# Where the two halves of an output projection run: beside the attention, or after it beside the norms

## The chip, the core and the metric

The kernel runs on one core of a Trainium2 chip. The metric is the device time of one execution in microseconds (us), median of the runs. A NeuronCore has TensorE (PE: matmuls and transposes; its weight loads are listed as PEld), VectorE (DVE), ScalarE (ACT), GpSimd (POOL) and SyncE (SP), which here issues the DMA transfers. Each engine works off its own queue in order and waits on semaphores.

## The reference, cut to what matters

One decoder layer over 1024 tokens and 16 meta tokens, d_model 1024. Two token mixers (retention, and sparse attention with a top-256 choice of keys) each give 512 columns; together they are mapped by one output projection, added to the residual, normed, and put through an MLP.

```python
y = jnp.concatenate([y_ret, y_dsa], axis=-1).astype(h.dtype)
h = h + y @ w_out[l]
u = rmsnorm(h, norm2_w[l]).astype(h.dtype)
h = h + jnp.square(jax.nn.relu(u @ w_ff1[l])) @ w_ff2[l]
```

All of it is in float32. The kernel reaches that precision with pairs: each operand is split into a high half (a float32r copy, made by ACT) and a low half (the rest, made by DVE or GpSimd), and a product is three matmuls, high by high, low by high and high by low.

## The kernel before

The tokens are eight blocks of 128 rows. The stages follow each other: norm and projections with the indexer and the top-k (0 to about 425 us), the attention (to about 652), the rest of the output projection with the second norm (to about 713), and the MLP (to the end). The MLP works with sums and differences of quarters of its operands (seven products in place of eight, names `u1` to `u7`), and reads W1 in pieces of 512 KB (`w1_load`, name `wr`), from which DVE makes sums (`sum`, L952) and ACT and DVE make halves (`wh`, `wl`, L955 and L956).

The attention runs in rounds `u` = 2 i + g, for block i and half g of the heads. In a round `attend_p` computes the scores and the softmax of (i, g), while `attend_v` of the round before transposes the probabilities (L607) and multiplies them by the values (L617, L619).

The output projection is cut into 16 pieces, (half of the columns, block). A piece needs `out_prep`, which loads the retention part of y from memory (`yr`), transposes it on PE (L654), and splits both parts into `ys` (ACT L657, and DVE or GpSimd L658); two sets of `ys` take turns. Then `out_mm` does 24 matmuls (L669 to L671), and DVE adds the residual `hp` and so drains the result (L674), which goes to memory as `hd`. `out_w` loads and splits half of the weights; only one half is held at a time. In what order the pieces come is said by a table, `pieces`, for the rounds, and by a list, `todo`, for the stretch after the attention:

```python
pieces = {4: [(0, 0)], 5: [(0, 1)], 7: [(0, 2)], 9: [(0, 3)], 10: [(1, 0)], 11: [(1, 1)], 12: [(1, 2)],
          13: [(1, 3)], 14: [(1, 4)], 15: [(1, 5)]}
...
todo = [(1, 7), (0, 4), (0, 5), (0, 6), (0, 7)]
```

Piece (1, 6) runs beside the last `attend_v`. So ten pieces and that one, eleven in all, lie within the attention, and five after it; the first half of the weights is loaded twice.

`norm2` turns a row block of h into operands of the MLP: a square with its sum on ACT (L852), a root on GpSimd (L142), the scaled row `un` on DVE (L854), eight transposes on PE (L862), and then halves of sums and differences. For blocks 0 to 3 that is light (two more instructions on DVE), for blocks 4 to 7 heavy (six more on DVE). Blocks 0 to 3 were normed beside the last `attend_v` (`norms_a`), blocks 4 to 7 in the stretch after it (`norm2_b`, `norm_step`). The first four products of the MLP (`u4` and `u2`, twice) need only blocks 0 to 3; the next one (`u3`) needs all eight.

The code is written with generators that `spread` takes in turns. A scheduler of the framework then sets the order of each engine's queue from its own forecast of times, so the order in the queues is not the one written; the section on the change shows it where it matters.

Of the kernel before, what the change touches and what calls it, by code (L numbers as in the profile page):

```python
# [18 lines left out]
D = 1024  # L19
# [3 lines left out]
NB = 8  # L23
# [58 lines left out]
def layer(ctx, tc, x, meta, norm1_w, w_in, ret_w, q_w, k_w, rel, w_out, norm2_w, w1, w2,  # L82
# [552 lines left out]
    hd = dr.tile([128, NB, D], F32, name="hd")  # L635

# [4 lines left out]
    def out_prep(ch, b):  # L641
        yr = wp.tile([128, 512], F32, tag="rl", name="yr", bufs=2)
        nc.sync.dma_start(yr, yrd[:, b])
# [6 lines left out]
        hp = at["hp"][oc[0] % 2]  # L650
        nc.sync.dma_start(hp, x[128 * b:128 * b + 128, 512 * ch:512 * ch + 512])
        tp = psB()
        for c in range(4):
            nc.tensor.transpose(tp[:, 128 * c:128 * c + 128], yr[:, 128 * c:128 * c + 128], ident)  # L654
        ys = [a.rearrange("p (c n) -> p c n", c=4) for a in at["y"][oc[0] % 2]]
        for k, src in enumerate((tp.rearrange("p (c n) -> p c n", c=4), ydsa[b])):
            nc.scalar.activation(ys[k], src, AF.Copy)  # L657
            (nc.gpsimd if k else nc.vector).tensor_tensor(ys[2 + k], src, ys[k].bitcast(F32), op=ALU.subtract)  # L658
        return ys, hp
# [4 lines left out]
    def out_mm(ch, b, ys, hp):  # L664
        hs, ls = ow[0]
        ps = psB()
        for d in range(8):
# [3 lines left out]
            nc.tensor.matmul(ps, yh, ls[d], start=False, stop=d == 7)  # L671
            yield
        dst = hrow[0][:, b % 2, :512] if b >= 4 and ch == 0 else hp
# [144 lines left out]
    while runs:  # L818
        for g in list(runs):
            try:  # L820
# [6 lines left out]
    pieces = {4: [(0, 0)], 5: [(0, 1)], 7: [(0, 2)], 9: [(0, 3)], 10: [(1, 0)], 11: [(1, 1)], 12: [(1, 2)],  # L827
              13: [(1, 3)], 14: [(1, 4)], 15: [(1, 5)]}
# [20 lines left out]
    def norm2(b, src, u):  # L849
# [20 lines left out]
        def temp():  # L870
            if b < 4:
                return wp.tile([128, 4, 128], F32, tag="wr", name="ut", bufs=3)
            return p2["p"].tile([128, 4, 128], F32, tag="yd", name="ut", bufs=4)
# [20 lines left out]
    def norms_a():  # L894
        nr = [page([128, 2, D], F32, "nr") for _ in range(2)]
        for b in range(4):
            nc.sync.dma_start(nr[b % 2][:, 0], hd[:, b])
            yield from norm2(b, nr[b % 2][:, 0], nr[b % 2][:, 1])
            yield

    spread((NB + 1, attend_v(NB - 1, 1)), (9, out_piece(1, 6)), (12, norms_a()))
# [10 lines left out]
    def load_h(b):  # L912
        nc.sync.dma_start(hrow[0][:, b % 2, 512:], hd[:, b, 512:])
# [213 lines left out]
    for k, (ch, b) in enumerate(todo):  # L1127
        if k == 1:
            out_w(0, True)
# [74 lines left out]
```

## Time and profile before

| | |
|---|---|
| median of 3 runs | 1323.49 us (1321.75 to 1327.82) |
| the profiled execution | 1322.03 us, span 1320.3 us |
| PE busy | 1254.5 us, 95% |
| DVE busy | 1038.5 us, 79% |
| ACT busy | 767.3 us, 58% |
| GpSimd busy | 253.5 us, 19% |
| mean granted TensorE clock | 0.986 |
| moved by DMA | 153.46 MB |

The span runs from the first to the last instruction; the profiled execution's own time is 1.7 us longer. PE's busy time counts the whole duration of matmuls that overlap in the array, so a full PE is read from the distance between starts. A granted clock of 1.00 is 2.4 GHz, 0.5 is 1.2 GHz.

### The profile page before, as it was taken

Reading aid. Unit: us, or ns where it says so; the run is one execution under the profiler, and the core shown is the slowest. Engines: PE = TensorE matmul, PEld = TensorE weight load, DVE = VectorE, ACT = ScalarE, POOL = GpSimd, SP = SyncE. Lnnn points to the kernel's source line nnn. Section 1 sums busy time; section 2 is a strip of 40 time slices with the busy share of each in tenths; the row PEclk is TensorE's granted clock in tenths of the full one; section 3 lists DMA queues with packets and bytes.
Section 4 is the critical chain, followed back from the end, with each engine's and each line's share of the span. In section 5 each row is a group of like instructions: output and inputs, shape, how many; then the busy total and the mean of one; then the engine's idle time right before and its main releaser. Section 6 shows DMA issues by size and latency. Waiting matters only on the chain. (4 is left out here: it accounts for less than half of the span.)

```text
span 1320.3 us, 18430 instructions
## 1 busy us (share of the span) xinstructions
PE 1254.5 (95%) x6144; PEld 1036.8 (79%) x6144; DVE 1038.5 (79%) x2277; ACT 767.3 (58%) x1588; POOL 253.5 (19%) x298
## 2 busy tenths in 40 slices
PE   5999989999999899999987999999999999999998
PEld 4888867877877677787775888888887888888887
DVE  5589999995458888776769877777778988887875
ACT  6567466887875668565746555554546444444442
POOL 4003472425335333210333000000000200000000
PEclk9999989999999999999997999999999999999999
DMA  8103031202112111212543343443538834444222
GB/s 275 59 17 90 22 91 63 72 9 72 35 55 74 66 62 56 65 47 74 179 149 112 141 159 131 150 159 131 177 144 303 342 141 168 151 144 177 94 96 96
DMA packets 94046, 153.46 MB, mean 116 GB/s; under 512 B 7752, under 2 KB 47856, under 8 KB 90240
## 3 DMA queue, kind: packets, MB, share of 16 engines
q1 hardware_dynamic: 93952, 152.29, 33.4%
q8 instruction: 48, 0.79, 0.2%
q14 instruction: 46, 0.38, 0.1%
HBM read 110.32 MB, written 43.46 MB: 116 GB/s over the span
## 5 line engine op out<-in xcount | busy, mean ns | idle before, releaser
L955 ACT ACTIVATE wh<-ga 128x512 fp32r<-128x512 f32 x144 | 87.3, 628 | 157.6 <-PE psB L1103 142.9
L246 PE MATMUL psA<-wh,uh 128*128 128x512 f32 x376 | 151.7, 404 | 3.5 <-DVE fg L481 2.2
L247 PE MATMUL psA<-wh,ul 128*128 128x512 f32 x376 | 149.2, 397 | 0.0
L248 PE MATMUL psA<-wl,uh 128*128 128x512 f32 x376 | 148.7, 396 | 0.0
L956 DVE TENSOR_TENSOR wl<-ga,wh 128x512 fp32r<-128x512 f32 x144 | 96.5, 686 | 47.4 <-ACT wh L955 46.8
L955 ACT ACTIVATE wh<-sum 128x512 fp32r<-128x512 f32 x128 | 78.7, 625 | 80.1 <-DVE sum L952 75.6
L723 ACT ACTIVATE jk_top<-sc,tcand 128x784 bf16<-128x784 f32 (+2 forms) x93 | 98.3, 1057 | 23.9 <-DVE tcand L793 19.8
L1103 PE MATMUL psB<-wh,wl 128*128 128x512 f32 x280 | 109.0, 389 | 0.9 <-DVE wl L956 0.9
L1104 PE MATMUL psB<-wl,wh 128*128 128x512 f32 x280 | 108.9, 389 | 0.0
L1102 PE MATMUL psB<-wh 128*128 128x512 f32 x280 | 106.8, 389 | 0.0
L956 DVE TENSOR_TENSOR wl<-sum,wh 128x512 fp32r<-128x512 f32 x128 | 87.5, 684 | 6.2 <-ACT wh L955 6.2
L246 PEld LDWEIGHTS psA<-wh,uh 128*128 128x128 f32 x376 | 71.3, 190 | 17.6 <-DVE fg L481 1.9
L1022 POOL COPY ga<-wl 128x1 f32<-128x1 f32 x8 | 6.6, 826 | 404.8 <-DVE wl L956 361.4
L248 PEld LDWEIGHTS psA<-wl,uh 128*128 128x128 f32 x376 | 71.2, 190 | 13.9
L247 PEld LDWEIGHTS psA<-wh,ul 128*128 128x128 f32 x376 | 71.4, 190 | 12.2
L718 DVE TENSOR_SCALAR_CACHE_REDUCE jk_cnt<-sc,tcand 128x400 bf16<-128x400 f32 (+2 forms) x93 | 70.3, 756 | 1.0
L194 POOL TENSOR_TENSOR wl<-wr,wh 128x512 fp32r<-128x512 f32 x48 | 67.0, 1418 | 18.4 <-ACT wh L189 12.3
L358 ACT ACTIVATE rl<-psB,absw 128x320 f32<-128x320 f32 (+5 forms) x104 | 53.0, 555 | 28.5 <-DVE sc L362 15.9
L1103 PE MATMUL psA<-wh,wl 128*128 128x512 f32 x168 | 65.4, 389 | 0.0
L1104 PE MATMUL psA<-wl,wh 128*128 128x512 f32 x168 | 65.4, 389 | 0.0
L1102 PE MATMUL psA<-wh 128*128 128x512 f32 x168 | 64.9, 389 | 0.0
L952 DVE TENSOR_TENSOR sum<-wr,wr 128x512 f32<-128x512 f32 x48 | 31.7, 686 | 41.5 <-DMA wr<-in_w_ff_dram 36.0
(392 smaller groups left out, 3642.7 us busy)
## 6 DMA issues: line engine op xcount, KB each, us to landing
ga<-hid SPq DMA_DIRECT2D x28, 1024.0 KB, 5.0
wr<-in_w_ff_dram SPq DMA_DIRECT2D x34, 512.0 KB, 5.0
hid<-hs SPq DMA_DIRECT2D x48, 256.0 KB, 2.0
wr<-in_w_in_dram SPq DMA_DIRECT2D x32, 256.0 KB, 3.1
gb<-in_w_ff_dram SPq DMA_DIRECT2D x8, 1024.0 KB, 5.0
ga<-in_w_ff_dram SPq DMA_DIRECT2D x8, 1024.0 KB, 5.9
wr<-in_w_out_dram SPq DMA_DIRECT2D x12, 512.0 KB, 4.1
xt<-in_x_dram SPq DMA_DIRECT2D x8, 512.0 KB, 4.4
```

The source lines that it names most:

```text
L194: e.tensor_tensor(shl, raw, shp.bitcast(F32), op=ALU.subtract)
L246: nc.tensor.matmul(ps[:P, :n], uh, wh, start=d == 0, stop=False)
L247: nc.tensor.matmul(ps[:P, :n], ul, wh, start=False, stop=False)
L248: nc.tensor.matmul(ps[:P, :n], uh, wl, start=False, stop=d == 7)
L358: nc.scalar.activation(r[:, :w], ps[:, :w], AF.Relu, scale=absw[:, i, h:h + 1])
L718: nc.vector.tensor_scalar(jk_[:, :ncol[i]], sc[i], cand[:, j:j + 1], 0.0, op0=ALU.is_ge, op1=ALU.add, accum_out=cnt[:, j:j + 1])
L723: nc.scalar.activation(jk_top[:, :ncol[i]], sc[i], AF.Sign, scale=-1.0, bias=cand[:, j:j + 1], accum_out=cnt[:, j:j + 1])
L955: nc.scalar.activation(view(hi), s, AF.Copy)
L956: nc.vector.tensor_tensor(view(lo), s, view(hi).bitcast(F32), op=SUB)
L1102: nc.tensor.matmul(ps[tb], ah[:, t], bh, start=j == 0 and m not in CONT, stop=False, skip_group_check=True)
L1103: nc.tensor.matmul(ps[tb], al[:, t], bh, start=False, stop=False, skip_group_check=True)
L1104: nc.tensor.matmul(ps[tb], ah[:, t], bl, start=False, stop=j == NO - 1, skip_group_check=True)
```

## The change

The first half of the columns is now done for all blocks before the second: blocks 0 to 5 within the attention (one piece in every second round), block 6 beside the last `attend_v`, and block 7 just after it. The second half follows for all eight blocks, beside the norms of all eight. Each half of the weights is loaded once. The pieces of the second half don't transpose and split y again: while the first half's `out_mm` runs, the four tiles of `ys` are stored to memory (`ysd`, 1 MB per block, L681), and `out_prep` of the second half loads them back (L664). The drain of the second half writes to `hrow` in place, and the first half of the row is fetched from `hd`. `norms_a` is gone. In the line numbers of the changed kernel the drain is L684, `un` is L863, the transposes of a norm are L871, and the heavy differences (`ut`) are L884.

```diff
     def out_prep(ch, b):
-        yr = wp.tile([128, 512], F32, tag="rl", name="yr", bufs=2)
-        nc.sync.dma_start(yr, yrd[:, b])
+
...
         hp = at["hp"][oc[0] % 2]
+        flat = at["y"][oc[0] % 2]
+        ys = [a.rearrange("p (c n) -> p c n", c=4) for a in flat]
+        if ch == 0:
+            yr = wp.tile([128, 512], F32, tag="rl", name="yr", bufs=2)
+            nc.sync.dma_start(yr, yrd[:, b])
+            tp = psB()
+            for c in range(4):
+                nc.tensor.transpose(tp[:, 128 * c:128 * c + 128], yr[:, 128 * c:128 * c + 128], ident)
+            for k, src in enumerate((tp.rearrange("p (c n) -> p c n", c=4), ydsa[b])):
+                nc.scalar.activation(ys[k], src, AF.Copy)
+                (nc.gpsimd if k else nc.vector).tensor_tensor(ys[2 + k], src, ys[k].bitcast(F32), op=ALU.subtract)
+        else:
+            for k in range(4):
+                nc.sync.dma_start(flat[k].bitcast(F32), ysd[:, b, k])
...
             nc.tensor.matmul(ps, yh, ls[d], start=False, stop=d == 7)
+            if ch == 0 and d == 5:
+                for k in range(4):
+                    nc.sync.dma_start(ysd[:, b, k], flat[k].bitcast(F32))
             yield
-        dst = hrow[0][:, b % 2, :512] if b >= 4 and ch == 0 else hp
+        dst = hrow[0][:, b % 2, 512:] if ch else hp
...
-    pieces = {4: [(0, 0)], 5: [(0, 1)], 7: [(0, 2)], 9: [(0, 3)], 10: [(1, 0)], 11: [(1, 1)], 12: [(1, 2)],
-              13: [(1, 3)], 14: [(1, 4)], 15: [(1, 5)]}
+    pieces = {4: [(0, 0)], 6: [(0, 1)], 8: [(0, 2)], 10: [(0, 3)], 12: [(0, 4)], 14: [(0, 5)]}
...
-    spread((NB + 1, attend_v(NB - 1, 1)), (9, out_piece(1, 6)), (12, norms_a()))
+    spread((NB + 1, attend_v(NB - 1, 1)), (9, out_piece(0, 6)))
...
-    todo = [(1, 7), (0, 4), (0, 5), (0, 6), (0, 7)]
+    todo = [(0, 7)] + [(1, b) for b in range(NB)]
     pre = out_prep(*todo[0])
     for k, (ch, b) in enumerate(todo):
         if k == 1:
-            out_w(0, True)
-        nxt = out_prep(*todo[k + 1]) if k < 4 else None
-        spread((8, out_mm(ch, b, *pre)), *([(1.3, norm_step(k + 2))] if k >= 2 else []))
+            out_w(1, True)
+        nxt = out_prep(*todo[k + 1]) if k < NB else None
+        spread((8, out_mm(ch, b, *pre)), *([(1.3, norm_step(b - 1))] if k >= 2 else []))
```

The order on DVE at the first drains that go to `hrow`, that is, of the first blocks that are normed after the attention. Before (the drains are those of blocks 4, 5 and 6; `wr_7814` and `wr_7826` are the second pair of W1 pieces):

```order
L674 TENSOR_TENSOR hrow<-psB,hp 128x512
L952 TENSOR_TENSOR sum<-wr_7814,wr_7826 128x512 x2
L674 TENSOR_TENSOR hrow<-psB,hp 128x512
L854 SCALAR_TENSOR_TENSOR un<-hrow,rs_y,nrow_2078 128x1024
L674 TENSOR_TENSOR hrow<-psB,hp 128x512
L854 SCALAR_TENSOR_TENSOR un<-hrow,rs_y,nrow_2078 128x1024
L877 TENSOR_TENSOR ut<-ut,psB 128x512
```

In the changed kernel, DVE at the same place (the drains are those of blocks 0, 1 and 2; `wr_7749` and `wr_7761` are the second pair):

```order
L684 TENSOR_TENSOR hrow<-psB,hp 128x512
L956 TENSOR_TENSOR wl<-sum,wh 128x512
L863 SCALAR_TENSOR_TENSOR un<-hrow,rs_y,nrow_2078 128x1024
L877 TENSOR_TENSOR u2l<-psB,u2h 128x4x128
L952 TENSOR_TENSOR sum<-wr_7749,wr_7761 128x512 x2
L884 TENSOR_TENSOR ut<-psB,f_7068 128x512
L684 TENSOR_TENSOR hrow<-psB,hp 128x512 x2
L863 SCALAR_TENSOR_TENSOR un<-hrow,rs_y,nrow_2078 128x1024 x2
```

The pair of `sum` now stands behind block 0's `un`, ahead of the drains of blocks 1 to 7.

DVE later, from the first heavy difference of block 4 to the drain of the last piece. Before:

```order
L877 TENSOR_TENSOR ut<-ut,psB 128x512
L877 TENSOR_TENSOR ut<-psB,f_7239 128x512
L956 TENSOR_TENSOR wl<-wr_7678,wh 128x512
L956 TENSOR_TENSOR wl<-sum,wh 128x512
L854 SCALAR_TENSOR_TENSOR un<-hrow,rs_y,nrow_2078 128x1024
L952 TENSOR_TENSOR sum<-wr_7814 128x512
L956 TENSOR_TENSOR wl<-wr_7826,wh 128x512
L956 TENSOR_TENSOR wl<-wr_7814,wh 128x512
L674 TENSOR_TENSOR hrow<-psB,hp 128x512
```

DVE in the changed kernel, from the same instruction to the same drain:

```order
L884 TENSOR_TENSOR ut<-ut,psB 128x512
L884 TENSOR_TENSOR ut<-psB,f_7068 128x512
L956 TENSOR_TENSOR wl<-wr_7620,wh 128x512
L863 SCALAR_TENSOR_TENSOR un<-hrow,rs_y,nrow_2078 128x1024
L956 TENSOR_TENSOR wl<-sum,wh 128x512
L956 TENSOR_TENSOR wl<-wr_7761,wh 128x512
L952 TENSOR_TENSOR sum<-wr_7749 128x512
L877 TENSOR_TENSOR u5l<-psB,u5h 128x4x128
L884 TENSOR_TENSOR ut<-psB,f_7069 128x512
L899 TENSOR_TENSOR f_7068<-psB,f_7068 128x512
L956 TENSOR_TENSOR wl<-wr_7749,wh 128x512
L684 TENSOR_TENSOR hrow<-psB,hp 128x512
```

The same work stands there in nearly the same order. From the first `ut<-ut,psB` (block 4) to the fourth (block 7) DVE's queue has 38 instructions before and 38 after.

SP's queue in the changed kernel, where the reloads of blocks 1 to 3 are issued:

```order
L943 DMA wr_7620<-in_w_ff_dram 128x4x256
L664 DMA ys<-ysd 128x512
L685 DMA hd<-hp 128x512
L943 DMA wr_7749<-in_w_ff_dram 128x4x256
L664 DMA ys<-ysd 128x512 x5
L943 DMA wr_7761<-in_w_ff_dram 128x4x256
L665 DMA hp<-in_x_dram 128x512
L685 DMA hd<-hrow 128x512
L665 DMA hp<-in_x_dram 128x512
L664 DMA ys<-ysd 128x512 x2
L913 DMA hrow<-hd 128x512
```

The reloads take turns with the W1 pieces, the residual and the stores of `hd`, which wait for drains on DVE; before, SP had 256 KB of `yr` per piece here and no transfer of `ys`.

## Rows read from the trace of the kernel before

**Rows 1.** The page: busy time by engine, and PE's granted clock in 40 slices.
```profile
PE 1254.5 (95%) x6144; PEld 1036.8 (79%) x6144; DVE 1038.5 (79%) x2277; ACT 767.3 (58%) x1588; POOL 253.5 (19%) x298
...
PEclk9999989999999999999997999999999999999999
```
**Rows 2.** Stretches: length, then busy time (and instructions) of each engine, clock, DMA.
```profile
660.00:675.00 15.00, 14.94 (x68) 12.05 (x67) 5.14 (x7) 5.84 (x10) 6.38 (x7) 1.00 0.50 163
...
690.00:705.00 15.00, 10.29 (x48) 7.91 (x47) 15.00 (x21) 9.81 (x18) 5.56 (x5) 0.85 0.44 153
...
800.00:900.00 100.00, 100.00 (x443) 82.84 (x442) 75.66 (x120) 52.29 (x95) 0.00 (x0) 1.00 0.42 149
```
**Rows 3.** Timeline of PE: start, duration, instruction, [wait before it and its releaser].
```profile
655.20 0.60 PE L654 MATMUL psB<-ident,yr 128*128 128x128 f32 x4
655.55 0.48 PE L669 MATMUL psB<-wh,ys 128*128 128x512 f32 x1
655.87 0.40 PE L670 MATMUL psB<-wh,ys 128*128 128x512 f32 x1
...
675.79 0.39 PE L671 MATMUL psB<-wl,ys 128*128 128x512 f32 x1
679.42 1.45 PE L862 MATMUL psB<-ident,un 128*128 128x128 f32 x8 [3.24 <-DVE un L854]
...
713.37 0.79 PE L984 MATMUL psB<-u3h,wh 128*128 128x512 f32 x1 [4.83 <-ACT u3h L867]
```
**Rows 4.** Timeline of DVE, 676 to 712.
```profile
676.28 1.29 DVE L952 TENSOR_TENSOR sum<-wr,wr 128x512 f32<-128x512 f32 x2 [3.51 <-issue]
...
678.09 1.27 DVE L854 SCALAR_TENSOR_TENSOR un<-hrow,rs_y,nrow 128x1024 f32<-128x1024 f32 x1
...
681.49 0.68 DVE L877 TENSOR_TENSOR ut<-ut,psB 128x512 f32<-128x512 f32 x1
...
684.53 0.69 DVE L956 TENSOR_TENSOR wl<-sum,wh 128x512 fp32r<-128x512 f32 x1 [1.17 <-ACT wh L955]
...
690.28 0.68 DVE L674 TENSOR_TENSOR hrow<-psB,hp 128x512 f32<-128x512 f32 x1
...
695.68 2.32 DVE L854 SCALAR_TENSOR_TENSOR un<-hrow,rs_y,nrow 128x1024 f32<-128x1024 f32 x1
...
711.98 0.67 DVE L877 TENSOR_TENSOR ut<-ut,psB 128x512 f32<-128x512 f32 x1
```
**Rows 5.** Stretches, each one round of the attention; columns as above.
```profile
480.82:489.11 8.29, 6.97 (x39) 5.02 (x38) 8.01 (x27) 7.42 (x17) 2.25 (x1) 1.00 0.21 65
...
513.12:531.68 18.56, 16.19 (x98) 13.19 (x96) 15.91 (x53) 15.47 (x32) 12.44 (x8) 1.00 0.23 80
...
546.87:563.38 16.51, 16.32 (x98) 13.93 (x98) 12.33 (x43) 10.05 (x20) 3.55 (x2) 1.00 0.14 47
...
580.48:600.00 19.52, 18.46 (x107) 15.32 (x106) 15.13 (x48) 13.12 (x25) 1.28 (x1) 1.00 0.22 72
```
**Rows 6.** Groups by line and shape: count, busy us and mean ns, idle before.
```profile
L658 POOL TENSOR_TENSOR ys<-yd,ys 128x512 fp32r<-128x512 f32 x16 | 21.4, 1339 | 74.4 <-ACT ys L657 74.4
...
L658 DVE TENSOR_TENSOR ys<-psB,ys 128x512 fp32r<-128x512 f32 x16 | 10.9, 686 | 2.8 <-ACT ys L657 2.7
...
L196 DVE SCALAR_TENSOR_TENSOR wl<-wr,rgain,wh 128x512 fp32r<-128x512 f32 x12 | 9.2, 781 | 1.8 <-ACT wh L189 1.7
...
L852 ACT ACTIVATE un<-hrow 128x1024 f32<-128x1024 f32 x4 | 4.2, 1058 | 5.8 <-DVE hrow L674 4.6 <-PE psB L862 0.8 <-DVE ut L877 0.4
```
**Rows 7.** DMA issues (KB, us to landing) at 640 to 720 and 985 to 1060; one stretch.
```profile
wr<-in_w_out_dram SPq DMA_DIRECT2D x4, 512.0 KB, 4.1
...
hrow<-hd SPq DMA_DIRECT2D x4, 256.0 KB, 4.2
...
m<-hd SPq DMA_DIRECT2D x4, 1024.0 KB, 10.2
...
1015.00:1020.00 5.00, 5.00 (x23) 4.13 (x23) 4.49 (x8) 2.20 (x4) 0.00 (x0) 1.00 1.05 428
```

More of the change, by code (lines that the diff above doesn't have):

```diff
@@ L635, in layer @@
     hd = dr.tile([128, NB, D], F32, name="hd")
+    ysd = dr.tile([128, NB, 4, 512], F32, name="ysd")
     ow = {}
@@ L650, in out_prep, with out_mm @@
         hp = at["hp"][oc[0] % 2]
-        nc.sync.dma_start(hp, x[128 * b:128 * b + 128, 512 * ch:512 * ch + 512])
[L652 to L659, printed above, removed]
+        flat = at["y"][oc[0] % 2]
[12 more added lines that the diff above has]
+                nc.sync.dma_start(flat[k].bitcast(F32), ysd[:, b, k])
+        nc.sync.dma_start(hp, x[128 * b:128 * b + 128, 512 * ch:512 * ch + 512])
+        return ys, hp, flat
     def out_w(ch, alt=False):
         ow[0] = load_cols(w_out, [(512 * ch, 512)], alt=alt, gain=rgain)
-    def out_mm(ch, b, ys, hp):
+    def out_mm(ch, b, ys, hp, flat):
         hs, ls = ow[0]
@@ L870, in temp @@
         def temp():
-            if b < 4:
-                return wp.tile([128, 4, 128], F32, tag="wr", name="ut", bufs=3)
             return p2["p"].tile([128, 4, 128], F32, tag="yd", name="ut", bufs=4)
@@ L892, in norm2 @@
             nc.vector.tensor_tensor(g1, tps[1], g1, op=ADD)
[L894 to L899, printed above, removed]
-    spread((NB + 1, attend_v(NB - 1, 1)), (9, out_piece(1, 6)), (12, norms_a()))
+    spread((NB + 1, attend_v(NB - 1, 1)), (9, out_piece(0, 6)))
     att.close()
@@ L912, in load_h @@
     def load_h(b):
-        nc.sync.dma_start(hrow[0][:, b % 2, 512:], hd[:, b, 512:])
+        nc.sync.dma_start(hrow[0][:, b % 2, :512], hd[:, b, :512])
     for m, pg_ in ((5, page), (3, page), (6, page_c), (7, page_c)):
@@ L918, in norm2_b @@
     def norm2_b(b):
-        if b == 4:
+        if b == 0:
             hrow.append(page([128, 2, D], F32, "un"))
@@ L1119, in norm_step @@
         yield
-        if b > 4:
+        if b > 0:
             for _ in norms.pop(b - 1):
@@ L1128, in layer @@
         if k == 1:
-            out_w(0, True)
-        nxt = out_prep(*todo[k + 1]) if k < 4 else None
-        spread((8, out_mm(ch, b, *pre)), *([(1.3, norm_step(k + 2))] if k >= 2 else []))
+            out_w(1, True)
+        nxt = out_prep(*todo[k + 1]) if k < NB else None
+        spread((8, out_mm(ch, b, *pre)), *([(1.3, norm_step(b - 1))] if k >= 2 else []))
         if k == 0:
-            load_h(4)
-            load_h(5)
+            load_h(0)
+            load_h(1)
         pre = nxt
-        if k == 2:
+        if k == 6:
             w1_load(0, 0)
```

## The prediction

> **What bounds the kernel now.** I read the page's engine row and clock slices first [rows 1]. TensorE (PE) is busy 95% of the span, and its granted clock dips twice, in the sixth slice (0.8) and, deeper, in the 22nd (0.7; a slice is 33 us, so 693 to 726). The table of stretches shows that second place from both sides [rows 2]: from 660 to 675 PE is full while VectorE (DVE) is busy 5.14 of 15 us; from 690 to 705 it is the other way round, DVE 15.00 of 15 and PE 10.29, at a clock of 0.85. By contrast 800 to 900 is what PE does undisturbed: 443 matmuls in 100 us, 0.226 us each. So a matmul's cost is the distance between two starts, not the 0.4 us of its row, and a piece (`out_mm`, 24 matmuls) costs 5.45 us.
>
> PE's own order shows the price of that place [rows 3]. After the matmul at 675.79 PE waits 3.24 us for `un`, the scaled row of block 4, and the eight transposes of that norm start at 679.42. From there to the first matmul that needs all eight norms (`u3`, at 713.37, after another wait of 4.83 us) pass 34.0 us, in which PE has 72 matmuls and 32 transposes, some 20 us of work. DVE shows why [rows 4]. At 676.28 it had stood 3.51 us at two `sum` of the first FFN weights, with drains and `un` behind them in its queue; and from 681.49, block 4's first difference, to 711.98, the same of block 7, it works through the norms of blocks 4 to 7 and the first weight operands. So that stretch is as long as DVE's work.
>
> Within the attention PE is the limit wherever a piece runs beside a round: 16.32 of 16.51 us. A round without a piece is DVE's: 8.01 busy of 8.29 us, 97%, against 6.97 of PE [rows 5].
>
> **The change, part by part.** *Transposes.* Eight of sixteen `out_prep` no longer transpose. Four transposes start at 655.20, the next matmul at 655.55, and the one after it comes 0.32 us on, not 0.23 [rows 3]: 0.44 us each, 3.5 us in all, on the engine that sets the end there. **-3.5**. The splits that go with them (DVE 0.69, GpSimd 1.34 us per block [rows 6], and two on ACT), and one of three loads and splits of half of `w_out`, lie beside PE work. By themselves I count them at nothing; without that cover DVE's part would be 8 x 0.69 = 5.5 us. Where they matter is DVE's load in the attention, below.
>
> *The first stall.* Before, the second pair of `sum` stands between the drains of the first two of four blocks. After, it stands behind block 0's `un`, ahead of the drains of all the other blocks, as the order shows; and PE's queue has 36 or 48 matmuls (8 us or more) between a block's last matmul and the transposes of its norm, for blocks 0 to 5. The norm's path is drain 0.68, square 1.06, a root on GpSimd and `un` 1.27 [rows 4, 6], some 4 us with the short instructions between. So the 3.24 us go: **-3.2**. Bounds: nothing, if another wait takes the place, and -3.2.
>
> *The tail.* From block 4's first difference to block 7's DVE has 38 instructions in its queue, before and after alike, two of them `un`. They took 30.5 us. Undisturbed (two `sum` take 1.29 us together, so some 0.61 from start to start; `un` 1.27) they would take 24.5; the rest went into longer ones, as `un` with 2.32 at 695.68, and into a wait of 1.2 us for a weight operand at 684.53. The matmuls and transposes that PE has after block 4's transposes are also the same number. What goes is the slow clock in those eight transposes, which follow an idle PE (their row is 1.45 us long, where four at full clock take 0.60 [rows 3]; eight would be some 1.05), and probably the wait, as those operands are ready earlier: -0.4 - 1.2, **-1.6**. Bounds -6.4 (DVE undisturbed and full clock) and 0.
>
> *The attention.* Four of eleven pieces leave it, three of them from the rounds of blocks 5 to 7. A round that loses its piece cannot shrink by the whole 5.9 us (5.45 + 0.44), since DVE then sets it, at 97% [rows 5]. Row of 546.87: PE 16.5 - 5.9 = 10.6; DVE 12.33 less a drain and a split (1.38) = 10.95, or 11.3 at 97%: +0.7. Row of 580.48: PE 18.46 - 5.9 = 12.6; DVE 13.75, or 14.2: +1.6. Row of 513.12: PE 10.3; DVE 15.91 - 1.38 - 2.3 (three `w_out` splits of 0.78 [rows 6], which leave this round too) = 12.2, or 12.6: +2.3; but PE idled 2.4 us in this round, where the halves of the weights were switched, and the switch is now elsewhere: 0. The fourth piece leaves a stretch after the last softmax, where other transposes and products fill PE: 0. Sum **+2.3**; bounds -2 (DVE's work spreads to neighbouring rounds) and +9 (each of three rounds shrinks by half of the 5.9 only).
>
> *The reload.* Each block of the second half fetches 1 MB in four transfers, into one of two sets. Two tiles of a set come free half-way through the piece before last, two at its end; each pair is needed 9.1 us after it came free (half a piece, 2.7, and a whole one with eight transposes, 6.4). In the stretch after the attention a 256 KB load took 4.2 us and one of 512 KB 4.1; later, in a crowded stretch, one of 1 MB took 10.2 [rows 7]. I take the former, which share the stretch: hidden, **0**. If that cover is gone each block waits: at 10.2 plus the 3.5 us that a drain was held on DVE (the queue's `hd` stores wait for drains, below), 4.6 x 7 = 32 us. Bounds 0 and +32. From the first piece of that stretch to the last reload some 17.6 MB move (7.3 of reloads, 1.0 of stores, 2.6 of weights, 6.7 of `x`, `hd` and `hrow`), in 48 us of PE work: 365 GB/s. The row of 1015 moved 428, so there is room, though little.
> The Trainium skill ("DMA: Bandwidth & Descriptors", Specifications) gives a core some 358 GB/s of HBM. By that page the 17.6 MB take 49 us, an estimate, 1 us more than PE's work, and the reloads would run late one after the other; the trace goes past that figure.
> The stores add 1 MB per piece in the attention, whose rows show a DMA share of 0.12 to 0.23: 0.
>
> Sum: -3.5 - 3.2 - 1.6 + 2.3 + 0 = -6.0 us. The profiled execution took 1322.0 us, so 1316.0; the median of the three runs is 1.5 us above it: **1317.5**. A measurement of this kernel tells 0.5% (6.6 us) from no change, so this lies just at that bound.
>
> **Rivals.**
> *DVE is undisturbed in the tail*: 4.8 us more than forecast, 1313, or 1308 with the attention at its good bound. For it speaks that DVE idles from 660 to 675 now and has the light norms to do there; against it that the 38 instructions are the same, with the same GpSimd splits beside them.
> *The stall only moves*: DVE takes its queue in order, and a drain or `un` behind a `sum`, or behind an operand of the norm before, holds PE ahead of another block's transposes. The 3.2 are not saved and the tail stays as it was: 1317.5 + 4.8 = 1322, no change.
> *The attention does not shrink*: +9 in place of +2.3: 1324, no change.
> *The reload comes late*: SyncE's queue issues in order, and reloads stand behind `hd` stores that wait for drains. Nothing is lost up to 9.1 us from a set's release; at 10.2 it is 7 x 1.1 = 8 us, 1325; beyond 10.9 the kernel is slower than before by more than 0.5%, and at 11.5 us, 17 us lost, it takes 1334. For it speak the 365 GB/s, against it the 4.1 and 4.2 us.
> *The change doesn't do what it says* would be halves still transposed twice or weights loaded three times; the order shows neither.
>
> **How the numbers follow.** Forecast 0.35 (1313 to 1321), undisturbed DVE 0.23, moved stall 0.16, attention 0.13, late reload 0.13. Faster by over 0.5%, below 1316.9, is the second case and half of the first: 0.40. Slower by over 0.5%, above 1330.1, is most of the last: 0.11. The rest, 0.49, is no change. The range goes from 1305, the undisturbed tail with the attention at its good bound and a little for what the rows don't show, to 1327, a reload late by some 10 us; the slower part of the last case stays outside.
>
> **What would show it.** Between the end of the attention and the end of the last piece PE should have no wait of over 1 us, at full clock. The first matmul on `u3` should follow block 4's transposes by some 32 us, and the first piece of that stretch should start some 25 us earlier than 652. Second-half pieces should have no transposes of `yr`. The forecast is wrong upward if PE waits for DMA or `ys` ahead of second-half pieces, or if rounds without a piece last longer than 1.03 of their DVE time; downward if the 32 us are near 27.

## The result and the profile after

The changed kernel takes **1312.9 us** (median of 6 runs, 1311.8 to 1318.0), the kernel before 1322.6 beside it: ratio **0.9943**, 95% interval 0.9927 to 0.996. On another chip it was 1314.3 against 1324.1, 0.9928 (0.990 to 0.9957). So 9.7 us were gained both times, against 6.0 forecast. The time lies inside the range and 4.6 us below its number, and the gain by the ratios, 0.57% and 0.72%, lies beyond the bound of 0.5%, where the forecast had put it just at the bound; both intervals reach down to 0.4%.

The page of the profile after: busy time by engine, and PE's granted clock (before: [rows 1]).

```profile
PE 1252.8 (96%) x6112; PEld 1035.4 (79%) x6112; DVE 1031.2 (79%) x2265; ACT 755.3 (58%) x1564; POOL 236.3 (18%) x286
...
PEclk8999989999999999999997999999999999999999
```

PE has 32 transposes fewer, DVE, ACT and GpSimd the splits of eight blocks and of one reload of weights fewer, and the deep dip of the clock has stayed in the 22nd slice.

To see where the 9.4 us between the two profiles went, I cut each span at two marks on PE that both kernels have: the four transposes (L623) that normalise a product of the attention, an early set of them and the last; and at the first `u3`. The table also has the last set but one, behind which only the last product is left. PE's timeline of the kernel before, at the marks:

```profile
460.45 0.49 PE L623 MATMUL psB<-ident,rs 128*128 128x128 f32 x3
649.43 0.60 PE L623 MATMUL psB<-ident,rs 128*128 128x128 f32 x4
```

The same of the changed kernel, with waits behind the attention (before: [rows 3]):

```profile
461.24 0.49 PE L623 MATMUL psB<-ident,rs 128*128 128x128 f32 x3
619.64 0.60 PE L623 MATMUL psB<-ident,rs 128*128 128x128 f32 x4
...
633.07 0.47 PE L676 MATMUL psB<-wh,ys 128*128 128x512 f32 x1 [0.92 <-DMA ys<-ysd]
642.62 0.50 PE L677 MATMUL psB<-wh,ys 128*128 128x512 f32 x1 [1.58 <-DMA ys<-ysd]
652.93 0.50 PE L676 MATMUL psB<-wh,ys 128*128 128x512 f32 x1 [1.15 <-DMA ys<-ysd]
674.89 1.03 PE L871 MATMUL psB<-ident,un 128*128 128x128 f32 x8
693.14 0.63 PE L871 MATMUL psB<-ident,un 128*128 128x128 f32 x4 [1.73 <-DVE un L863]
...
705.47 0.79 PE L984 MATMUL psB<-u3h,wh 128*128 128x512 f32 x1 [3.47 <-ACT u3h L876]
```

| stretch, us | before | after | after, profiled again |
|---|---|---|---|
| to the early mark | 460.5 | 461.2 | 461.2 |
| early mark to last but one (rounds) | 165.7 | 143.1 | 144.6 |
| last but one to last (last product) | 23.3 | 15.3 | 15.4 |
| both together (attention) | 189.0 | 158.4 | 160.0 |
| last mark to first `u3` | 63.9 | 85.8 | 86.1 |
| first `u3` to the end | 606.9 | 605.4 | 606.7 |

The attention repeats well: of the nine profiles of kernels with the changed attention seven have 158.3 to 158.4 us for it and two have 160.0; the two profiles with the old one have 188.8 and 189.0.

The eight norm transposes of block 4 at 674.89 have no wait any more: the first stall, 3.24 us, is gone. In its place stand three waits for reloads, 3.65 us together. From block 4's transposes to `u3`, the tail, it takes 30.6 us instead of 34.0. The stretch behind `u3` differs by 1.5 us in one profile and by 0.2 in the other, so that is not the change's.

Why the reloads are late is read from SyncE's timeline. The store of block 7's last tiles (L681) cannot be issued before GpSimd has split them, up to 629.27.

```profile
629.39 0.50 SPq L681 DMA_DIRECT2D ysd<-ys  x1
629.98 0.38 SPq L664 DMA_DIRECT2D ys<-ysd  x1
630.42 0.47 SPq L681 DMA_DIRECT2D ysd<-ys  x1
630.94 0.56 SPq L664 DMA_DIRECT2D ys<-ysd  x1
631.89 0.54 SPq L943 DMA_DIRECT2D wr<-in_w_ff_dram  x1
635.76 0.32 SPq L664 DMA_DIRECT2D ys<-ysd  x1
636.17 0.39 SPq L685 DMA_DIRECT2D hd<-hp  x1
636.66 0.38 SPq L943 DMA_DIRECT2D wr<-in_w_ff_dram  x1
637.09 2.64 SPq L664 DMA_DIRECT2D ys<-ysd  x5
```

Block 1 uses those tiles next. The load at 635.76 is for one of them; it waited 3.3 us for the store to land, and the next, behind a store and a weight load, was issued at 637.09 and held PE until 642.62. The same stretch by windows (length, busy time and count of PE, PEld, DVE, ACT, POOL, clock, DMA share, GB/s) shows that the transfers also fill the DMA engines:

```profile
635.00:640.00 5.00, 5.00 (x24) 4.14 (x23) 1.01 (x2) 0.23 (x1) 0.00 (x0) 1.00 1.05 385
...
645.00:650.00 5.00, 5.00 (x27) 4.21 (x26) 2.99 (x5) 2.04 (x4) 0.00 (x0) 1.00 1.05 387
```

385 and 387 GB/s lie above the 358 that the Trainium skill ("DMA: Bandwidth & Descriptors", Specifications) gives a core of HBM, and the reloads were late all the same, some by bytes and some by order.

### The profile page after: what moved, and what is told of

Same layout as the page of the kernel before. It is cut to its first block, busy times and chain, and to the rows that moved or that the text cites. A ratio compares the mean times of both kernels' runs of the same rounds, so it can differ in the third digit from the quotient of the medians.

```text
span 1310.9 us, 18438 instructions
## 1 busy us (share of the span) xinstructions
PE 1252.8 (96%) x6112; PEld 1035.4 (79%) x6112; DVE 1031.2 (79%) x2265; ACT 755.3 (58%) x1564; POOL 236.3 (18%) x286
## 4 chain that ended last, share of the span: by engine, by line
PE 65%; DVE 20%; ACT 6%; issue 4%; DMA 3%; POOL 1%; SPq 0%; ACTq 0%; DVEq 0%; POOLq 0%
PE psB L1103 5%; PE psB L1104 5%; PE psB L1102 5%; ACT jk_top L733 4%; PE psB L984 4%; PE psA L984 4%; PE psB L985 4%; PE psB L986 4%; PE psA L985 4%; PE psA L986 4%; DVE jk_cnt L728 3%; PE psA L246 3%; PE psA L1103 3%; PE psA L247 3%; PE psA L1104 3%
## 5 line engine op out<-in xcount | busy, mean ns | idle before, releaser
L955 ACT ACTIVATE wh<-sum 128x512 fp32r<-128x512 f32 x128 | 78.6, 625 | 84.2 <-DVE sum L952 69.5
L194 POOL TENSOR_TENSOR wl<-wr,wh 128x512 fp32r<-128x512 f32 x44 | 61.1, 1411 | 16.3 <-ACT wh L189 13.6
L615 ACT ACTIVATE ph<-psB 128x512 fp32r<-128x512 f32 x72 | 41.5, 594 | 39.1 <-PE psB L607 28.1
```

Source lines behind the costliest of these rows:

```text
L955: nc.scalar.activation(view(hi), s, AF.Copy)
```

## The experiments

**The waits for reloads: weight loads out of the way.**

```
+        if gi == 0:
+            nc.gpsimd.tensor_copy(raw[:, 0, 0:1], hrow[0][:, 1, 512:513])
-        if k == 6:
+        if k == 4:
             w1_load(0, 0)
```

> The changed kernel, with the first two loads of the first FFN weights tied behind block 3's drain of the second half (a one-column GpSimd copy into each tile), so that no weight load stands between the first reloads. In the changed kernel TensorE waits 3.65 us for reloads, in three waits (0.92, 1.58, 1.15). Theory A, the weight loads get in the reloads' way, in SyncE's queue and as bytes: the three waits fall below 1.5 us together, and from the first matmul of block 7's first half to block 4's norm transposes it takes about 51 us in place of 53.1. Since three sums and one lower half of these weights then come later on VectorE, the tail (block 4's transposes to the first u3 matmul) grows by up to 4 x 0.61 = 2.4 us from 30.6: 1312 to 1314 us in all. Theory B, what is late is block 7's first half, whose tiles must be stored before they are filled again: the wait of 1.58 stays, the sum of waits is 2.5 or more, and with the longer tail the kernel takes 1314 to 1316 us.

Measured: 1315.0 us, ratio to before 0.994 (0.9917 to 0.9963), the same as the changed kernel. Two waits are left, 0.81 and 1.17; that of 1.58 is gone. Their sum, 1.98, lies between the bounds of the two theories, 1.5 and 2.5. The two stretches, last mark to block 4's transposes and from there to `u3`, in windows (columns as above) of this kernel:

```profile
618.03:668.65 50.62, 48.32 (x228) 38.65 (x227) 26.88 (x34) 22.75 (x42) 14.21 (x21) 1.00 0.92 304
668.65:704.24 35.59, 25.93 (x117) 20.40 (x116) 33.33 (x43) 21.70 (x40) 12.61 (x12) 0.88 0.45 158
```

and of the changed kernel:

```profile
619.64:674.89 55.25, 51.27 (x240) 40.80 (x239) 28.51 (x37) 22.98 (x42) 14.23 (x20) 1.00 0.91 310
674.89:705.47 30.58, 22.90 (x105) 18.11 (x104) 29.84 (x42) 22.20 (x41) 13.10 (x10) 0.87 0.35 121
```

The first stretch got 4.6 us shorter and the second 5.0 longer; the sum is 86.2 against 85.8. Twelve matmuls, 2.7 us, only passed from the first stretch to the second. Theory A is right about the middle wait and wrong about its worth. DVE is 94% busy in the second stretch (98% in the changed kernel), which speaks for DVE setting when `u3` starts.

**A third set of tiles, fetched two pieces ahead.** `fetch` issues the four loads of one block. In this version block 7's are issued ahead of block 5's piece, into the same set of tiles, so that block 5's product is not taken from its own numbers; the transfers and instructions are those meant, but that one fetch comes a piece early.

```
-        flat = at["y"][oc[0] % 2]
+        flat = at["y"][(1, 2, 0, 1, 2, 0, 1, 0)[b] if ch else oc[0] % 2]
...
+    third = page_c([128, 4, 512], F32R, "ys3")
...
+        for b_ in ((0, 1) if k == 0 else (k + 1,)):
+            fetch(b_)
```

> The changed kernel with a third set of four tiles for the reloads of the second half (in a page that the last u7 tile needs only later), fetched two pieces ahead, in the order in which the tiles are used. Theory A, a set is filled again too shortly before it is read: the reload waits of TensorE fall from 3.65 us to 0.5 or less, nothing else moves, and the kernel takes 1309 to 1310 us. Theory B, the 16 DMA engines are full between 635 and 655 (share 1.02 to 1.05), so the bytes of this stretch set its length whatever is fetched ahead: 2 us or more of waits are left, 1311 to 1313 us.

Measured: 1316.8 us, 0.9954 (0.9935 to 0.9972). The waits fall to 1.22 and 0.19 us, 1.41 in all, between the two theories' bounds of 0.5 and 2; the time lies above both. From the last mark to `u3` it takes 85.1 us, 0.8 less than without. Both experiments say the same: with 1.7 and 2.2 of the 3.65 us of waits gone, `u3` hardly moves.

**The trip through memory left out.**

```
-            for k in range(4):
-                nc.sync.dma_start(flat[k].bitcast(F32), ysd[:, b, k])
+            nc.sync.dma_start(yr, yrd[:, b])
+            nc.sync.dma_start(flat[3].bitcast(F32), ysd[:, b, 0])
...
+            for k, src in enumerate((tp.rearrange("p (c n) -> p c n", c=4), ys[3].bitcast(F32))):
+                nc.scalar.activation(ys[k], src, AF.Copy)
```

> The changed kernel without its halves in memory: only the half of y that VectorE leaves on chip is stored (256 KB a block instead of 1 MB), and the second half of the columns loads both halves of y (512 KB), transposes one and splits both again, as the kernel before did. All else (order of pieces and norms) as in the changed kernel. It prices the trip through memory alone. By my sum the transposes come back, 8 x 0.44 = +3.5 us, and the reload waits go, -3.65, so about 1313 us, no difference: the trip through memory gave back what it saved. VectorE's eight splits of 0.69 lie in a stretch in which it is busy 27 of 53 us: 0. Rival 1: the waits don't come from the bytes, 2 us or more of them stay, 1315 to 1317. Rival 2: the splits hold TensorE up (GpSimd's 1.3 to 1.7 us each ahead of a second half of a piece), one wait of 0.3 to 1 us per block, 1315 to 1320.

Measured: 1319.1 us, 0.9969 (0.9953 to 0.9985), some 5 us slower than the changed kernel. From the last mark to `u3`: 92.5 us, +6.7. PE's timeline of this kernel at block 1:

```profile
649.59 0.50 PE L683 MATMUL psB<-wh,ys 128*128 128x512 f32 x1 [2.78 <-ACT ys L670]
651.34 0.79 PE L684 MATMUL psB<-wh,ys 128*128 128x512 f32 x1 [1.25 <-POOL ys L671]
651.93 0.63 PE L685 MATMUL psB<-wl,ys 128*128 128x512 f32 x1
652.36 0.63 PE L683 MATMUL psB<-wh,ys 128*128 128x512 f32 x1
```

The reload waits are gone and two for the splits have come, near rival 2 though for one block only: 0.6 us more of waits in all up to block 4's transposes (4.6 against 4.0). Behind them PE runs at half clock to 656.20, ten matmuls 0.43 us apart in place of 0.23: +2.0, and 0.4 on a set of transposes. The rest, some 3.7, is close to the forecast's 8 x 0.44 of transposes. The half clock is of a kind that differs between executions, as the last section shows. So the halves in memory are worth 3 to 7 us here, not nothing.

**The first stall alone, in the kernel before.**

```
+        if gi == 0:
+            nc.gpsimd.tensor_copy(raw[:, 0, 0:1], hrow[0][:, 0, 0:1])
```

> The kernel before, with its first two loads of the first FFN weights tied behind block 4's drain (a one-column GpSimd copy into each tile), so that the two sums at which VectorE stood 3.51 us no longer lie ahead of block 4's drain and norm; their order on VectorE is then drain, drain, un, drain, un, two differences, sum. This is the first stall alone. My term: TensorE's wait of 3.24 us ahead of block 4's transposes falls below 0.5, and from the last stretch's first piece (652.0) to those transposes it takes 24.2 us in place of 27.4. Three sums and a lower half move behind it into the tail, +4 x 0.61 = 2.4 us at most, so the kernel takes 1320 to 1322 us, against 1322.6. Rival, the stall only moves: another wait of 2.5 us or more stands ahead of the first u3 matmul beyond those 2.4 us, and the kernel takes 1323 us or more.

Measured: 1318.4 us, 0.998 (0.9965 to 0.9996). PE's timeline of this kernel:

```profile
675.84 1.03 PE L862 MATMUL psB<-ident,un 128*128 128x128 f32 x8
...
709.34 0.79 PE L986 MATMUL psB<-u3h,wh 128*128 128x512 f32 x1 [6.83 <-ACT u3h L867]
```

No wait is left ahead of block 4's transposes, which come 3.6 us earlier than in [rows 3], the tail is 33.5 us where it was 34.0, and `u3` starts 4.0 us earlier. Median against median 3.5 us are gained, by the ratio 2.6. My term (3.2) holds, and the stall did not move. It also says that a third of the change's gain was to be had without it.

**DVE and GpSimd in the tail, both ways.** Eight subtractions from DVE to GpSimd:

```
-            total(7, tps[1], g2, ADD, nc.vector)
+            total(7, tps[1], g2, ADD, nc.gpsimd)
-            nc.vector.tensor_tensor(U[1][1][:, :, s], f1 ...
+            nc.gpsimd.tensor_tensor(U[1][1][:, :, s], f1 ...
```

> The changed kernel with eight subtractions of the norms' end moved from VectorE to GpSimd: the four u7l and the four u1l. Five of them stand on VectorE before block 7's first difference, from which the first u3 matmul follows. Theory D, VectorE's queue sets the time from block 4's norm transposes to the first u3 matmul: 30.6 - 5 x 0.61 = 27.5 us there, and 1309 to 1310 us in all. Rival P, the two engines slow each other: VectorE's un took 2.30 us instead of 1.28 wherever GpSimd's subtractions ran beside it, so as much is lost as is moved: 29.5 us or more there, 1312 to 1314. Rival L, the chain through the last pieces (drain, square, root, un, transposes) sets it and VectorE's other work only fills: no change, 30.6.

Measured: 1318.7 us, 0.9955 (0.9938 to 0.9972). The tail is 33.6 us, 3.0 longer instead of 3.0 shorter. And twelve the other way, `u4l`, `u3l` and `u6l` from `nc.gpsimd` to `nc.vector` in the same function:

> The changed kernel with the norms' twelve subtractions u4l, u3l and u6l taken from GpSimd to VectorE, the other way round from the experiment that moved eight to GpSimd. In the changed kernel's tail six of them stand ahead of block 7's first difference. Theory P (the two engines slow each other): seven VectorE instructions beside them took 5.9 us more there than their like elsewhere (un 2.30 and 2.34 against 1.28, wl 1.78 against 0.68), about 1.0 us for each of GpSimd's six, and on VectorE itself one costs 0.61; so the tail falls from 30.6 by 6 x 0.4 = 2.4, to some 28 us, and the kernel to 1310 to 1312. Theory D, VectorE's count alone sets the tail: 6 x 0.61 more, 34 us, 1316 to 1318.

Measured: 1318.8 us (one of six executions took 4357 us, and the ratio is without it), 0.9956 (0.9933 to 0.9979); tail 32.4 us. Neither way helps, and the rows say why. DVE's timeline of the changed kernel, GpSimd's splits being at work from 678.3 to 681.8 and from 689.1 to 694.1:

```profile
678.32 2.34 DVE L863 SCALAR_TENSOR_TENSOR un<-hrow,rs_y,nrow 128x1024 f32<-128x1024 f32 x1
680.58 1.78 DVE L956 TENSOR_TENSOR wl<-sum,wh 128x512 fp32r<-128x512 f32 x1
...
690.09 0.68 DVE L952 TENSOR_TENSOR sum<-wr,wr 128x512 f32<-128x512 f32 x1
690.69 2.30 DVE L863 SCALAR_TENSOR_TENSOR un<-hrow,rs_y,nrow 128x1024 f32<-128x1024 f32 x1
...
693.51 0.67 DVE L884 TENSOR_TENSOR ut<-psB,f 128x512 f32<-128x512 f32 x1
```

GpSimd in the changed kernel:

```profile
689.10 2.81 POOL L877 TENSOR_TENSOR u3l<-ut,u3h 128x512 fp32r<-128x512 f32 x1 [0.33 <-ACT u3h L876]
```

and DVE of the kernel with the twelve on DVE:

```profile
679.32 1.28 DVE L863 SCALAR_TENSOR_TENSOR un<-hrow,rs_y,nrow 128x1024 f32<-128x1024 f32 x1
...
681.11 0.69 DVE L956 TENSOR_TENSOR wl<-sum,wh 128x512 fp32r<-128x512 f32 x1
...
691.25 1.28 DVE L863 SCALAR_TENSOR_TENSOR un<-hrow,rs_y,nrow 128x1024 f32<-128x1024 f32 x1 [0.44 <-POOL rs_y L142]
```

Without GpSimd's subtractions none of DVE's 47 instructions from block 4's first difference to block 7's is long. With them only those are long that read two operands from SBUF, the core's own memory (`un`, `wl`, `u7l`); one with an operand in PSUM, where PE's products land (`ut<-psB,f`), took 0.67 beside a GpSimd split. Nor is each of the former long: `sum` at 690.09 took 0.68 beside a GpSimd split, which for its part took 2.81 where others took 1.30. The Trainium skill ("SBUF — State Buffer", Who interferes with whom) says this: a DVE instruction with two SBUF inputs contends with a GpSimd instruction that reads SBUF; one with at most one such input, outside the modes in which DVE uses two ports, does not. The trace agrees. Theory P is shown as the mechanism, but its sum was half the truth: from block 4's first difference to block 7's DVE now has 46 instructions before the last, 9 more than the 37 of the changed kernel (6 moved, 3 that the new order brought along), 5.4 us, against 4.1 us of lengthening that went; 0.4 more of waits make up the rest.

**The attention's rounds.** Three minima over 128x512 in each of three rounds, nine in all, 0.68 us each in the trace. They were meant for rounds without a piece; but the `attend_v` of (4, 1), (5, 1) and (6, 1) runs in rounds 10, 12 and 14, which have one in the changed kernel:

```
+            if (i, g) in ((4, 1), (5, 1), (6, 1)) and k in (1, 2, 3):
...
+                nc.vector.tensor_reduce(jk1, ph.bitcast(F32), axis=mybir.AxisListType.X, op=ALU.min)
```

> The changed kernel with three more VectorE instructions (a minimum over 128x512 of a tile already on chip, into a column that nobody reads, some 0.6 us each) in each of the rounds that have no piece late in the attention: rounds 10, 12 and 14 of the attention, 9 in all, 5.4 us of VectorE. My forecast held such a round to be VectorE's, so that it could not shrink by a whole piece. Theory F (forecast): VectorE sets these rounds, and from the attention's third product normalisation to its last the time grows by 4 us or more. Theory S: VectorE's queue runs ahead and behind across rounds and is free on the whole (131 of 162 us busy), TensorE sets the stretch: it grows by 1.5 us or less.

Measured: 1319.8 us, 0.9961 (0.9945 to 0.9978). From the early mark to the last it takes 165.1 us against 158.4 (160.0 in the repeat), +6.7 or +5.1 for 6.1 us of DVE. That is theory F's growth, and where it lies is telling. Cut at every mark from the early one to the last but one, the five rounds with a piece take 78.5 us against 78.6, though the minima stand in three of them; the six without take 71.0 against 64.8. One without a piece, first in this kernel and then in the changed one, by windows (columns as above):

```profile
560.29:576.98 16.69, 16.22 (x94) 12.40 (x93) 16.50 (x67) 14.02 (x27) 5.81 (x3) 1.00 0.17 64
564.45:578.50 14.05, 13.98 (x87) 12.03 (x86) 13.83 (x51) 11.52 (x21) 1.30 (x1) 1.00 0.05 20
```

The reading is that DVE carries its work over from a round with a piece into the next without one, and sets the time there (99% busy). (The scheduler also laid the neighbouring rounds in another order.)

Two pieces out of the rounds:

```
-    ... 10: [(0, 3)], 12: [(0, 4)], 14: [(0, 5)]}
+    ... 10: [(0, 3)]}
+    def three():
+        for b in (4, 5, 6):
+            yield from out_piece(0, b)
-    spread((NB + 1, attend_v(NB - 1, 1)), (9, out_piece(0, 6)))
+    spread((NB + 1, attend_v(NB - 1, 1)), (27, three()))
```

> The changed kernel with two more pieces taken out of the attention: those of blocks 4 and 5 (first half) are done together with block 6's beside the last product, behind the last softmax, instead of in the late rounds of the attention. All work stays. It asks once more what my attention term asked: how much a round shrinks that loses its piece. By the forecast's rule (the round becomes VectorE's busy time at 97%), from the profile of the changed kernel: the round of 544.28 has 12.61 of VectorE, less a drain and a split of 1.38, which is 11.6 us, against 15.28 - 5.9 = 9.4: +2.2; the stretch from 570.32 to 600 gives 22.7 against 23.8: 0. Theory F (the rule holds): from the attention's fifth product normalisation to block 4's norm transposes (213.7 us in the first profile of the changed kernel, 215.4 in the second) it takes 216 to 219 us. Theory S (what VectorE has left over spreads to the rounds beside it): 213 to 215.5. A gain would say that pieces are cheaper outside than inside.

Measured: 1317.9 us, 0.9965 (0.9949 to 0.9981), 3 to 5 us slower than the changed kernel, as theory F has it. But its profile, which is its fastest run (1313.8), has 215.3 us in the stretch named, which is theory S. Cut at the last mark but one, that profile too speaks for theory F. The rounds of this kernel, up to that mark:

```profile
459.16:592.48 133.32, 126.33 (x756) 101.61 (x754) 116.94 (x388) 94.96 (x188) 26.60 (x14) 1.00 0.19 64
```

They take 9.8 us less than the changed kernel's 143.1, for 11.8 of pieces, so 2.0 are lost, where the forecast's rule gives 2.2. The sum hides it: the last product, with two pieces more, takes 29.1 us instead of 15.3, but from the last mark to block 4's transposes it takes 52.9 instead of 55.3, with 1.17 of reload waits left. The runs between 1317 and 1320 have no profile.

One piece taken out of the rounds of the kernel before, with the switch of the columns moved:

```
-pieces = {... 10: [(1, 0)], 11: [(1, 1)], 12: [(1, 2)], 13: [(1, 3)], 14: [(1, 4)], 15: [(1, 5)]}
+pieces = {... 11: [(1, 0)], 12: [(1, 1)], 13: [(1, 2)], 14: [(1, 3)], 15: [(1, 4)]}
...
+    def two():
+        for b in (5, 6):
+            yield from out_piece(1, b)
+    spread((NB + 1, attend_v(NB - 1, 1)), (18, two()), (12, norms_a()))
```

> The kernel before, with the switch from the first to the second half of the columns one round later, in a round that loads no query block: its pieces of the second half sit in rounds 11 to 15 (blocks 0 to 4), and blocks 5 and 6 are done beside the last product. One piece thereby leaves the late rounds for the end. In the kernel before TensorE waited 1.76 us for a query block whose load stood in SyncE's queue behind a load of w_out, which waited 6.2 us for a buffer, and a store that waited 8.1 us for its drain; my attention term counted that round at 0. Theory Q (that wait was one of the attention's losses that the change removed): no wait of TensorE for a query block is left there, and from the attention's fifth product normalisation to its last the time falls from 189.0 us (188.8 in the repeat with late weights) to 187.5 or less, and the kernel takes 1320 to 1321. Rival (the rounds make it up, VectorE being as late): 188.5 or more, no change in all.

Measured: 1329.7 us against 1322.8, 1.005 (1.0033 to 1.0067). The wait for the query block is gone, and yet the stretch between the marks has 195.9 us, 6.9 more, beyond both theories. PE's timeline of this kernel, at the mark one before the last, and behind it:

```profile
623.45 0.60 PE L623 MATMUL psB<-ident,rs 128*128 128x128 f32 x4
...
639.12 1.07 PE L862 MATMUL psB<-ident,nr 128*128 128x128 f32 x8 [2.12 <-DVE nr L854]
...
644.41 0.49 PE L617 MATMUL psB<-ph,vv 128*128 128x512 f32 x1 [1.51 <-ACT ph L615]
...
658.38 0.60 PE L623 MATMUL psB<-ident,rs 128*128 128x128 f32 x4
```

Up to that mark the rounds take 161.0 us (from 462.46) where they took 165.7 (460.45 to 626.15): 4.7 less, though a piece of 5.9 us and a wait of 1.8 had left them, so 3.0 were lost, by the forecast's rule. The last stretch grew by 11.7 us for 5.9 of work, with new waits of 2.12 and 1.51. Theory Q is refuted as a gain: the wait goes, and others take more.

**The heavy norms spread out.**

```
+    SEQ = (0, 4, 1, 5, 2, 6, 3, 7)
-    todo = [(0, 7)] + [(1, b) for b in range(NB)]
+    todo = [(0, 7)] + [(1, b) for b in SEQ]
```

The norms, `hrow` and `load_h` also go by place in `SEQ`.

> The changed kernel with the second half of the columns taken in the order of blocks 0, 4, 1, 5, 2, 6, 3, 7 instead of 0 to 7, and the norms with it. The norms of blocks 4 to 7 are the heavy ones on VectorE (two u-halves, four differences and sums and f, against one and one); in the changed kernel all four fall behind the reloads, where VectorE is full (29.8 of 30.6 us) and TensorE waits 7.7 us and then runs 21 matmuls at half clock (4.5 us); ahead of that VectorE is busy 27 of 53 us. Theory D (VectorE's pile of heavy norms sets the end of this stretch): three of them move into its idle time, some 3 x 4.5 us of VectorE, so the time from the attention's last product to the first u3 matmul falls by 5 to 9 us from 85.8, and the kernel takes 1304 to 1308 us. Rival L (the chain of the last block: drain, norm, transposes, its differences, the u3 halves, behind the last piece): at most 2 us are gained, 1311 to 1313. Rival R: reloads become late, as the order of the stored blocks doesn't matter to them they should not; with waits of over 4 us this would show, 1313 or more.

Measured: **1310.8 us**, 0.9894 (0.9866 to 0.9922), against 1314.3 for the changed kernel on the same chip. The gain is there, the mechanism not as expected: from the last mark to `u3` it takes 86.9 us, no less. But when `u3` starts, PE no longer waits for it and is at full clock. Windows of this kernel, up to `u3` and from there:

```profile
689.40:693.80 4.40, 4.40 (x10) 3.24 (x11) 4.40 (x4) 1.04 (x2) 2.44 (x2) 0.50 0.00 0
693.80:705.45 11.65, 9.64 (x46) 7.62 (x46) 11.65 (x18) 7.59 (x14) 4.72 (x3) 1.00 0.55 180
705.45:711.00 5.55, 5.55 (x26) 4.62 (x25) 5.55 (x10) 5.04 (x11) 0.77 (x1) 1.00 0.13 50
```

and of the changed kernel:

```profile
697.30:705.47 8.17, 4.67 (x12) 3.41 (x13) 8.17 (x13) 6.38 (x12) 1.89 (x2) 0.71 0.22 83
705.47:711.00 5.53, 5.53 (x13) 4.37 (x14) 5.53 (x9) 3.53 (x7) 2.89 (x2) 0.50 0.12 47
```

Behind the same 705.5 us PE does 26 matmuls against 13 in 5.5 us (17 in the changed kernel's second profile), since no last wait for `u3h` (3.47 us) stands ahead of it, after which the changed kernel's clock is 0.50; the waits of this kernel lie earlier, and ten matmuls at half clock with them. DVE is full from 690 on here too, so it probably still sets when `u3` starts; it only holds up less of PE's work.

With the twelve subtractions on DVE as well:

> The alternating order of blocks in the second half (0, 4, 1, 5, 2, 6, 3, 7), which took 1310.8 us, together with the norms' subtractions on VectorE. By theory P the two add up: 2 to 3 us below the alternating order, 1307 to 1309. By theory D it is slower than the alternating order by some 3 us, 1313 to 1315.

Measured: 1309.3 us, 0.9893 (0.9873 to 0.9914): in ratio the same as the alternating order alone, so neither theory's sum comes out. From the fifth set of norm transposes (here block 2's) to `u3` it takes 28.1 us instead of 30.7, and the stretch behind `u3` 604.1 instead of 603.1; PE again does 26 matmuls in the first 5.5 us of it. In their medians and ratios both versions lie below both kernels.

**The changed kernel again.**

> The changed kernel once more, for how far a stretch of one profile repeats in another. Expected: the time from the attention's last product to the first u3 matmul within 0.5 us of 85.8, the three reload waits within 0.5 us of 3.65 together, the rest behind the first u3 matmul within 1.5 us of 605.4, and the time up to the attention within 2 us. A larger change of the reload waits would mean that they are chance.

Measured: 1314.3 us; last mark to `u3` 86.1, waits for reloads 1.22, 1.62 and 1.07, so these are no chance.

## Why the prediction came out as it did

*Transposes (-3.5).* Right as far as shown: putting them back costs 6.7 us, of which 3.7 are left for them when the waits and the slow clock that come with them are taken off.

*The first stall (-3.2).* Right: the wait is gone, and removed by itself it gives 3.5 us. The rival by which it only moves is out.

*The tail (-1.6).* Right in kind, too small: 30.6 us where I forecast 32 and had 34.0. The matmuls and DVE's 38 instructions are the same, as I counted; they took 27.9 us from the first start to the last in place of 30.5. Of this 0.9 is waits (1.17 before, 0.27 now), and 1.7 that fewer were lengthened by GpSimd (5.8 us over their usual length before, 4.1 now). The other 0.8 lie between the transposes and the first difference, 0.4 of them the slow clock. I had taken the lengthening as constant. It depends on which instruction happens to stand beside a GpSimd split. So the rival with DVE undisturbed (1313) has its time by luck and not by its mechanism: `un` still takes 2.30.

*The attention (+2.3).* This term failed, in sign, and not in the rounds. Between the early and the last mark PE has 97 matmuls and 48 transposes less, 16 of them of the four pieces and 32 of the norms of blocks 0 to 3: 22.0 us, and 4.3 to 5.3 at 0.09 to 0.11 each, 26.3 to 27.3. The stretch is 30.6 us shorter, 29.0 in the repeat (and the first piece behind it starts at 621.83, 30 us earlier than 652 and not 25). So the term is between -1.7 and -4.3. The last mark but one divides it; the rounds and then the last product of the kernel before, by windows:

```profile
460.45:626.15 165.70, 157.73 (x923) 130.47 (x921) 128.69 (x404) 105.58 (x208) 39.33 (x25) 1.00 0.19 61
626.15:649.43 23.28, 20.63 (x119) 15.71 (x118) 17.05 (x26) 17.93 (x36) 8.73 (x10) 1.00 0.34 114
```

and of the changed kernel:

```profile
461.24:604.31 143.07, 135.88 (x811) 111.31 (x810) 119.72 (x392) 96.78 (x191) 27.87 (x15) 1.00 0.24 82
604.31:619.64 15.33, 14.63 (x85) 11.88 (x84) 9.01 (x15) 6.72 (x13) 0.00 (x0) 1.00 0.28 98
```

All four pieces left ahead of the last mark but one: 112 instructions of PE, 23.2 to 23.6 us. That part is 22.6 us shorter, 21.1 in the repeat, so 0.6 to 1.0 were lost there, 2.1 to 2.5 in the repeat. That has the forecast's sign, and a wait of 1.76 us for a query block, which I had not counted, went with them. The rule behind the term, that a round without a piece is DVE's, is borne out by six more microseconds of DVE (+6.2, all in such rounds), by the two pieces taken out (2.0 lost) and by the one taken out in the kernel before (3.0 lost).

What failed is the end, which I put at nothing: the stretch behind the last softmax, where "other transposes and products fill PE". Its last part, the last product, kept a piece and lost `norms_a`, 34 instructions of PE, 32 of them transposes, some 3 us; and it became 8.0 us shorter, 7.9 in the repeat. There PE had waited 2.5 us, mostly for `ph`, which ACT and DVE make, and now waits 0.7; DVE's work fell from 17.05 to 9.01 us and ACT's from 17.93 to 6.72. So 4 to 5 us came from taking the norms of blocks 0 to 3 away from the last product. That their work on ACT and DVE had held PE up is read from these rows; no run moved the norms alone.

*The reload (0).* Its step failed: the cover of 9.1 us forgot that block 1 reloads into tiles which block 7's first half must first store, and that a load takes 5.5 us in a stretch with full DMA engines, not 4.2. PE waits 3.65 us, which the text had named as a sign that it is wrong upward. But as the two experiments on it show, taking 1.7 and 2.2 of them away gains at most 0.8 at `u3`, since the tail, full of DVE's work, grows instead. In the sum the term was nearly right, by luck.

Adding up, against the first profile after: the attention is 5.6 to 6.6 us better than forecast, the tail 1.8, the end of the span 1.5 (chance, by the repeat), the start 0.8 worse and the reloads 3.65 worse by their rows. That makes 4.5 to 5.5, where 3.4 are to be explained (a profiled gain of 9.4 against 6.0); a microsecond or two stays open.

## What to carry to other kernels

When work leaves stretches that two engines share, price every stretch that loses work, also one in which the bounding engine looks full: the last product lost 3 us of PE's work and became 8 us shorter. Take neighbouring rounds together, since a second engine carries its work over from one to the next. A wait on the bounding engine is worth removing only if what stands behind it is not already waiting for a second engine: 1.7 and 2.2 us of waits were removed, and `u3` moved by +0.4 and -0.8. And when a heavy part comes in a row at the end, alternate it with the light part before counting instructions on its engine.

## What the runs showed of the hardware that was not expected

DVE instructions with two operands in SBUF take up to 1.1 us more beside a GpSimd subtraction (2.30 against 1.28, 1.78 against 0.68), or the subtraction itself is the longer one (2.81 against 1.30). So a subtraction moved to GpSimd (1.3 to 1.7 us there) can cost DVE more than the 0.6 us that it saves.

The clock after a wait differs between executions of one program. In both profiles of the changed kernel PE waits for `pm`, 1.65 and 1.64 us, and goes on with the same instructions; in windows, first the one:

```profile
585.20:587.90 2.70, 2.70 (x15) 2.23 (x14) 1.55 (x3) 1.06 (x3) 0.00 (x0) 1.00 0.01 3
```

and then the other:

```profile
585.50:588.30 2.80, 2.80 (x9) 2.23 (x8) 1.55 (x3) 0.72 (x2) 0.00 (x0) 0.51 0.01 3
```

The second has nine matmuls where the first has fifteen. That makes up the 1.6 us by which the two attentions differ, and differences of this size between single profiles say nothing of a change.
